# Two gate tiles by seven products, later reloads in a down projection, and a rearranged end in a one-layer decoder step

## The chip, the cores and the metric

The kernel runs on one core of a Trainium2 chip. A core has a matrix engine (TensorE, PE in the rows), a vector engine (VectorE, DVE), an activation engine (ScalarE, ACT), GpSimd (POOL), and SyncE (SP), whose queue issues most of the transfers between the chip's main memory and the core's on-chip memory. The engines run their own instruction lists in order and meet only at semaphores. The metric is the device time of one execution in microseconds (us), as the median of several; lower is better.

## The reference: what is computed

One layer of a decoder is applied to 16 meta tokens and 512 prompt tokens, and to 8 running sequences of 4 tokens each (32 sample tokens): 560 columns in all, with 1024 features. The layer is a half-step SwiGLU network, a mixer, and a second half-step SwiGLU network, each between two normalisations. Cut to what matters:

```python
h = x + 0.5 * rms_norm(swiglu(rms_norm(x, g1), w_gate, w_up, w_down), post1)
u = rms_norm(h, mix_pre_g)
q_a, k_a, v_a, gk_low, r_a, q_b, k_b, v_b, gate_a, gate_b = split(u @ w_in)
o_a = rms_norm(gla(q_a, k_a, v_a, gk_low), gla_norm_g) * silu(r_a)
o_b = stick_breaking_attention(q_b, k_b, v_b, cached pages)
m = sigmoid(gate_a) * (o_a @ w_o_gla) + sigmoid(gate_b) * (o_b @ w_o_sb)
h = h + rms_norm(m @ w_out, mix_post_g)
y = h + 0.5 * rms_norm(swiglu(rms_norm(h, g2), w_gate2, w_up2, w_down2), post2)
```

The hidden width is 2816. Cached keys and values lie in pages of 128 tokens, two for each sequence, found through a page table.

## The kernel before

**Layout.** Activations are held transposed: 128 features in the partitions, tokens in the columns. A weight tile is 128 output features by 1024 input features, which is eight 128x128 blocks. All products are made to nearly full float32 precision out of a rounded part (hi) and a remainder (lo) of both operands: hi*hi + hi*lo + lo*hi, three matmuls for each block. ScalarE makes the hi of a weight chunk (`Chunks.split`, L661, or `parted`, L959) and VectorE the lo (`tt`, whose one line is L153). Three buffers of each kind rotate: `raw` as it comes from memory, `hi` and `lo`. A raw buffer is free for the next transfer when its lo is made.

**Plain and seven-product tiles.** A plain tile ("R", `tile_steps`, L682 to L685) runs eight steps of six matmuls, the columns cut in two halves of 280 and 264. A pair of tiles can instead be made together by a Strassen-Winograd scheme ("S", `seven_steps`, L1028 to L1030): the weights of the pair are four quarters, VectorE makes four sums of them (`weight_sums`), sums of activation quarters are used beside the plain quarters, and seven products of 12 matmuls (272 columns) replace eight. Products 1 to 4 go to four accumulators a, d, b, c; products 5, 6 and 7 are added onto a, d and c. Before that, ScalarE has to copy a and d out, and VectorE has to add c into the sum called v. Four further adds make the pair's results. The first network and the second use the same scheme for most tiles, and so does one pair of each down product (`Down.pair`).

**Steps.** The code is written as a list of PE steps. `later(n, f)` puts f behind the n-th step from now; `when(n, f)` puts it behind step n of a stage. So the order of the instructions on PE, VectorE, ScalarE and GpSimd is written by hand; SyncE's order is set by a planner. Within a step the `later` work stands ahead of the `when` work.

**Rooms.** On-chip buffers come from an arena (`take`, `give`) that knows only the order of the program: a room taken again makes its new user wait for the last reader of the old one.

**The first down product** (`order1`, L1624 on). After two plain tiles comes the seven-product pair 2 and 3, then the first column halves of tiles 4 to 7, 22 steps of three matmuls each, then the second halves of tiles 7 to 4. Each tile's weights come as three chunks of 512, 448 and 448 KB. Right behind the pair, `h_again(8)` reloads the residual h, which was parked in memory, as eight transfers of 280 KB, one every eight steps (L1294). `EARLY = {4: 2}` fetches one 512 KB chunk of `w_in` ahead of its time when tile 4 starts (L634). The residual is first used when the first halves are normalised, 13 steps after tile 7's first half.

**The mixer's end** (`MIXER`, L2525 on). Steps 0 to 40 are r gates, 40 to 104 the product `o_a @ w_o_gla` (tiles o), then plain gate tiles a0 and a1 (8 steps each, `gate_a`), then S pairs and p tiles. Meanwhile the sampled tokens' attention uses pages gathered by GpSimd (`page`, L2069) into twelve rooms of a list `ring`; used pages go back to `ring`, and its rooms go back to the arena at step 113. `sample_out` copies its result out at steps 117 and 119 (16 small VectorE copies, L2254). The activation sums that the S pairs need were parked in memory: `sums_back` reloads them (L2342), at the steps of `SUMS_BACK`, and ScalarE and VectorE split them 8 to 12 steps later. From two steps after b0 starts, `obs` splits (L2348; a ScalarE rounding and a VectorE remainder each) follow every four steps.

**The end** (`Last.end`). Behind the last product, 256 prompt rows and the 32 sample rows remain. PE turns them by transposes, sums of squares are made by ones-matmuls (L855, L856), ScalarE makes the scale (L857, L858), VectorE scales and adds, and SyncE writes out. `tt(..., eng)` is `Last.add`'s helper; it takes VectorE unless told otherwise.

Of the kernel before, what the change touches and what calls it, by code (L numbers as in the profile page):

```python
# [121 lines left out]
def hybrid_step(  # L122
# [579 lines left out]
    GATES, ROWS, EARLY = 6, 1, {4: 2}  # L702
# [69 lines left out]
    class Last:  # L772
# [9 lines left out]
        def tile(self, n, h, acc):  # L782
# [13 lines left out]
            S.activation(q, acc[:, :w], AF.Square)  # L796
            y = self.view(g)[:, n % 3, c]
            if h and self.n[h] == KD:
                V.tensor_scalar(out=y, in0=acc[:, :w], scalar1=self.post[:, n : n + 1], scalar2=None, op0=ALU.mult)
            else:  # L800
                S.activation(y, acc[:, :w], AF.Copy, scale=self.post[:, n : n + 1])
# [13 lines left out]
        def add(self, g, c, rs):  # L815
            n = len(Norm.SETS[g])
            y, x = self.view(g)[:, :, c], hT_room[g].rearrange("p (k t) -> p k t", t=NT)[:, :n, c]
            tt(y, y, rs.unsqueeze(1).to_broadcast([P, n, c.stop - c.start]), ALU.mult)
            tt(x, x, y, ALU.add)

        def end(self, prompt, samples):
            def turned(src, c, n, w):
                p = ps("acc")
# [10 lines left out]
            def x_turned(c):  # L834
                t = take(D)
                for w in range(2):
                    p = ps()
                    for i in range(4):
                        T.transpose(p[:, P * i : P * i + P], hT[4 * w + i][:, c : c + P], ident)
                    S.copy(t[:, 512 * w : 512 * w + 512], p)  # L840
                return t
# [7 lines left out]
            q, rs = self.q["sum"], take(P)  # L849
# [4 lines left out]
            for i, c in enumerate((A, B)):  # L854
                T.matmul(p[:, i : i + 1], q[:, c : c + P], ones[:, :1], start=True, stop=True)  # L855
            T.matmul(p[:, 2 : 2 + NS], ones, q[:, C:NW], start=True, stop=True)  # L856
            S.activation(rs[:, : 2 + NS], p[:, : 2 + NS], AF.Ln, bias=epst, scale=1.0 / D)  # L857
            S.activation(rs[:, : 2 + NS], rs[:, : 2 + NS], AF.Exp, scale=-0.5)  # L858
            ya.append(turned(y_at, A, P, 1))
            out(A, 0, ya[0], xa, rs[:, 0:1])  # L860
            xb = x_turned(B)
            out(A, 1, ya[1], xa, rs[:, 0:1])
            for g in range(3):
                self.add(g, slice(C, NW), rs[:, 2 : 2 + NS])
            yb = [turned(y_at, B, P, w) for w in range(2)]
            pc = [turned(x_at, C, NS, w) for w in range(2)]
            out(B, 0, yb[0], xb, rs[:, 1:2])
            for w in range(2):
                t = take(512)
                S.copy(t[:NS], pc[w][:NS])  # L870
                nc.sync.dma_start(samples[:, 512 * w : 512 * w + 512], t[:NS])
            out(B, 1, yb[1], xb, rs[:, 1:2])
# [417 lines left out]
    def h_again(every):  # L1290
        nonlocal hT_room
        hT[:], hT_room = whole(KD)
        for k in range(KD):
            later(1 + every * k, lambda k=k: nc.sync.dma_start(hT[k], h_dram[k]))  # L1294
# [163 lines left out]
    with tc.manual_schedule(engines={E.PE, E.DVE, E.Activation, E.Pool}):  # L1458
# [607 lines left out]

    def page(src, i, c):
# [44 lines left out]
    def sample_keys(b, q, kp, kT):  # L2112
# [8 lines left out]
        if q:  # L2121
            ring.extend((kp[b, 0], kp[b, 1]))
# [88 lines left out]
    def sample_values(c, b0, vp, oz):  # L2211
# [8 lines left out]
        ring.extend(vp.values())  # L2220
# [83 lines left out]
    def gate_a(n):  # L2304
        acc = yield from tile_steps(um, W1)
        sg = take(NW)

        def sig():
            for h in range(2):
                S.activation(sg[:, h * HW : h * HW + W2[h]], acc[h][:, : W2[h]], AF.Sigmoid)  # L2310

# [390 lines left out]
```

## Time and profile before

| | |
|---|---|
| median of 3 runs | 1506.71 us (1506.67 to 1508.04) |
| the profiled execution: its time | 1508.72 us |
| its span, first to last instruction | 1507.0 us |
| PE busy | 1494.2 us of the span (99%) |
| VectorE busy | 1090.0 us (72%) |
| ScalarE busy | 771.5 us (51%) |
| GpSimd busy | 149.3 us (10%) |
| mean granted PE clock | 0.999 of full speed |
| data moved | 180.4 MB, mean 120 GB/s |

In timeline rows the columns are start, duration, engine, line, operation, output and inputs, shape and count, and in brackets the idle time before it and who ended it. Matmuls are pipelined, so their pace is read from the distance of two starts and not from a duration. In rows of windows the columns are the stretch, its length, busy time and instruction count of PE, weight loads, VectorE, ScalarE and GpSimd, then the granted PE clock, the busy share of the transfer engines and GB/s.

### The profile page before, as it was taken

What the parts mean: (1) busy time and instruction counts of PE and PEld (TensorE: products, weight loads), DVE (VectorE), ACT (ScalarE), POOL (GpSimd) and SP (SyncE); (2) the same over time, 40 slices, a digit from 0 to 9 for tenths busy, and PEclk for the clock granted to TensorE, in tenths of its full rate; (3) what the DMA queues carried; (4) which work ended last, traced back from release to release, by engine and by line L of the source; (5) the groups of instructions that cost most, each with busy time, mean ns of one, the idle gap of its engine ahead of it and who ended that gap; (6) DMA issues with size and microseconds to landing.
All of it is one profiled execution on the core that took longest, in us unless ns stands there. A gap on an engine that the chain in (4) does not pass through costs nothing.

```text
span 1507.0 us, 29698 instructions
## 1 busy us (share of the span) xinstructions
PE 1494.2 (99%) x11941; PEld 1442.1 (96%) x11941; DVE 1090.0 (72%) x1939; ACT 771.5 (51%) x1422; POOL 149.3 (10%) x216
## 2 busy tenths in 40 slices
PE   9999999999999999999999999999999999999998
PEld 8999999999999889999888899999999999999998
DVE  5888888853787866877776534977567898888544
ACT  6545454533655556565555343634564555455334
POOL 2000000000000011123324551000000000000000
PEclk9999999999999999999999999999999999999999
DMA  8123333336565473335555568335532233333352
GB/s 250 55 86 99 99 98 97 88 101 195 147 160 148 122 112 85 91 82 118 131 105 139 169 204 192 105 96 144 152 103 79 85 111 99 99 99 89 86 168 98
DMA packets 276458, 180.40 MB, mean 120 GB/s; under 512 B 10154, under 2 KB 260736, under 8 KB 276320
## 3 DMA queue, kind: packets, MB, share of 16 engines
q1 hardware_dynamic: 270864, 161.64, 40.6%
q0 software_dynamic: 5440, 16.85, 3.2%
q8 instruction: 94, 1.54, 0.4%
q14 instruction: 44, 0.36, 0.1%
q10 hardware_dynamic: 16, 0.00, 0.0%
HBM read 155.72 MB, written 22.74 MB: 118 GB/s over the span
## 4 chain that ended last, share of the span: by engine, by line
PE 94%; DVE 2%; DMA 2%; ACT 1%; issue 0%; DVEq 0%; SPq 0%; ACTq 0%
PE acc L682 8%; PE acc L1248 8%; PE acc L1249 8%; PE acc L685 8%; PE acc L683 8%; PE acc L1250 8%; PE acc L695 7%; PE acc L698 7%; PE acc L696 7%; PE acc L1191 2%; PE acc L1188 2%; PE acc L1189 2%; PE acc L1028 1%; PE acc L1029 1%; PE acc L1030 1%; PE ps L2023 1%
## 5 line engine op out<-in xcount | busy, mean ns | idle before, releaser
L153 DVE TENSOR_TENSOR lo<-raw,hi 128x1024 fp32r<-128x1024 f32 (+1 forms) x213 | 254.9, 1197 | 125.9 <-ACT hi L661 102.5
L153 DVE TENSOR_TENSOR room<-room,room 128x544 f32<-128x544 f32 (+17 forms) x413 | 259.0, 649 | 81.4 <-ACT room L740 15.0
L682 PE MATMUL acc<-room,hi 128*128 128x280 f32 (+1 forms) x928 | 271.2, 309 | 0.2 <-DVE room L156 0.2
L1249 PE MATMUL acc<-room,hi 128*128 128x280 f32 (+1 forms) x896 | 259.3, 289 | 0.0
L1248 PE MATMUL acc<-room,hi 128*128 128x280 f32 (+1 forms) x896 | 259.3, 289 | 0.0
L1250 PE MATMUL acc<-room,lo 128*128 128x280 f32 (+1 forms) x896 | 259.1, 289 | 0.0
L683 PE MATMUL acc<-room,hi 128*128 128x280 f32 (+1 forms) x928 | 250.3, 289 | 0.1
L685 PE MATMUL acc<-room,lo 128*128 128x280 f32 (+1 forms) x928 | 192.8, 289 | 0.0
L682 PEld LDWEIGHTS acc<-room,hi 128*128 128x128 f32 x928 | 174.7, 188 | 13.1 <-issue 11.0
L683 PEld LDWEIGHTS acc<-room,hi 128*128 128x128 f32 x928 | 175.0, 189 | 2.8 <-issue 1.9
L1248 PEld LDWEIGHTS acc<-room,hi 128*128 128x128 f32 x896 | 168.6, 188 | 0.0
L1250 PEld LDWEIGHTS acc<-room,lo 128*128 128x128 f32 x896 | 168.6, 188 | 0.0
L1249 PEld LDWEIGHTS acc<-room,hi 128*128 128x128 f32 x896 | 168.4, 188 | 0.0
L959 ACT CAST hi<-raw 128x1024 fp32r<-128x1024 f32 x92 | 96.4, 1052 | 133.1 <-PE acc L1249 48.8
L661 ACT CAST hi<-raw 128x1024 fp32r<-128x1024 f32 (+1 forms) x121 | 122.7, 1015 | 72.0 <-DMA raw<-in_ffn_w_down_dram 18.6
L685 PEld LDWEIGHTS acc<-room,lo 128*128 128x128 f32 x928 | 145.0, 188 | 0.0
L695 PE MATMUL acc<-room,hi 128*128 128x280 f32 (+2 forms) x498 | 143.7, 296 | 0.9 <-ACT hi L661 0.9
L696 PE MATMUL acc<-room,hi 128*128 128x280 f32 (+2 forms) x498 | 141.5, 292 | 0.0
L698 PE MATMUL acc<-room,lo 128*128 128x280 f32 (+2 forms) x498 | 128.4, 292 | 0.7 <-DVE lo L153 0.7
L959 ACT CAST hi<-room 128x1024 fp32r<-128x1024 f32 x84 | 70.2, 836 | 80.8 <-PE acc L1249 60.3
L695 PE MATMUL acc<-room,room 128*128 128x280 f32 (+3 forms) x366 | 107.8, 295 | 0.0
L153 DVE TENSOR_TENSOR lo<-room,hi 128x1024 fp32r<-128x1024 f32 x84 | 80.2, 955 | 36.7 <-ACT hi L959 36.5
(406 smaller groups left out, 3299.5 us busy)
## 6 DMA issues: line engine op xcount, KB each, us to landing
raw<-in_w_in_dram SPq DMA_DIRECT2D x49, 512.0 KB
raw<-in_ffn_w_down_dram SPq DMA_DIRECT2D x40, 448.0 KB
raw<-in_ffn_w_gate_dram SPq DMA_DIRECT2D x64, 256.0 KB
raw<-in_ffn_w_up_dram SPq DMA_DIRECT2D x64, 256.0 KB
out_dram<-room SPq DMA_DIRECT2D x36, 256.0 KB
raw<-in_ffn_w_down_dram SPq DMA_DIRECT2D x14, 512.0 KB
raw<-in_w_in_dram SPq DMA_DIRECT2D x28, 256.0 KB
h_dram<-room SPq DMA_DIRECT2D x24, 280.0 KB
```

The lines of the kernel that those rows point to most:

```text
L153: (eng or V).tensor_tensor(out=out, in0=a, in1=b, op=op)
L661: S.copy(h_, src)
L682: T.matmul(acc[h][:, : wid[h]], hi[k], a[h][0], start=(k == 0), stop=False)
L683: T.matmul(acc[h][:, : wid[h]], hi[k], a[h][1], start=False, stop=False)
L685: T.matmul(acc[h][:, : wid[h]], lo[k], a[h][0], start=False, stop=(k == KD - 1))
L695: T.matmul(acc[h][:nw, : wid[h]], wh, a[h][0], start=(k == 0), stop=False)
L696: T.matmul(acc[h][:nw, : wid[h]], wh, a[h][1], start=False, stop=False)
L698: T.matmul(acc[h][:nw, : wid[h]], wl, a[h][0], start=False, stop=(k == kt - 1))
L959: S.copy(hi[:, :kt], src)
L1248: T.matmul(x[:, :QW], hi, act[k][0], start=(first and k == 0), stop=False, skip_group_check=True)
L1249: T.matmul(x[:, :QW], hi, act[k][1], start=False, stop=False, skip_group_check=True)
L1250: T.matmul(x[:, :QW], lo, act[k][0], start=False, stop=(k == 3), skip_group_check=True)
```

## The change

- Gate tiles a0 and a1 become one S pair; the mixer is two steps shorter from there. `gate_a` goes. As no gate needs them any more, halves of the plain activations are given back when tile o0 starts (`halved`).
- `SUMS_BACK` moves from steps 80, 88, 96, 104 to 70, 78, 86, 92.
- Page rooms are given to the arena one by one once nothing is left to gather (`back`).
- In the first down product the eight loads of h start at step 24 and come every 11 steps; the early chunk of `w_in` is fetched when tile 5 starts. In the second one the loads of h start at step 8 and come every 5 steps.
- In the end, the sums of squares over all but the last tile are summed across partitions first, and the last tile's are added in PSUM by three further matmuls in place of a VectorE add. The sample rows are scaled and added on GpSimd; their transposes, copies and writes come last, and the writes are issued by ScalarE's queue.

```diff
-SUMS_BACK = (80, 88, 96, 104)
+SUMS_BACK = (70, 78, 86, 92)
-MIXER += [("R", "o", n) for n in range(8)] + [("R", "a", 0), ("R", "a", 1), ("S", "b", 0), ("S", "a", 2), ("S", "b", 2), ("R", "p", 0), ("R", "p", 1)]
+MIXER += [("R", "o", n) for n in range(8)] + [("S", "a", 0), ("S", "b", 0), ("S", "a", 2), ("S", "b", 2), ("R", "p", 0), ("R", "p", 1)]
...
-    GATES, ROWS, EARLY = 6, 1, {4: 2}
+    GATES, ROWS, EARLY = 6, 1, {5: 2}
...
-        def add(self, g, c, rs):
+        def add(self, g, c, rs, eng=None):
...
-            tt(y, y, rs.unsqueeze(1).to_broadcast([P, n, c.stop - c.start]), ALU.mult)
-            tt(x, x, y, ALU.add)
+            tt(y, y, rs.unsqueeze(1).to_broadcast([P, n, c.stop - c.start]), ALU.mult, eng)
+            tt(x, x, y, ALU.add, eng)
...
+            def x_turned(t, c, w):
+                S.copy(t[:, 512 * w : 512 * w + 512], turned(x_at, c, P, w, ps()))
+
+            def sums(p, q, first):
+                for i, c in enumerate((A, B)):
+                    T.matmul(p[:, i : i + 1], q[:, c : c + P], ones[:, :1], start=first and i == 0, stop=False, skip_group_check=True)
+                T.matmul(p[:, 2 : 2 + NS], ones, q[:, C:NW], start=False, stop=not first, skip_group_check=True)
...
-            xa = x_turned(A)
-            tt(q[:, A:NW], q[:, A:NW], self.q["last"][:, A:NW], ALU.add)
-            ya = [turned(y_at, A, P, 0)]
...
+            sums(p, self.q["sum"], True)
+            x_turned(xa, A, 0)
+            sums(p, self.q["last"], False)
             S.activation(rs[:, : 2 + NS], p[:, : 2 + NS], AF.Ln, bias=epst, scale=1.0 / D)
             S.activation(rs[:, : 2 + NS], rs[:, : 2 + NS], AF.Exp, scale=-0.5)
-            ya.append(turned(y_at, A, P, 1))
-            out(A, 0, ya[0], xa, rs[:, 0:1])
-            xb = x_turned(B)
-            out(A, 1, ya[1], xa, rs[:, 0:1])
             for g in range(3):
-                self.add(g, slice(C, NW), rs[:, 2 : 2 + NS])
+                self.add(g, slice(C, NW), rs[:, 2 : 2 + NS], G)
+            x_turned(xa, A, 1)
+            ya = [turned(y_at, A, P, w) for w in range(2)]
+            for w in range(2):
+                out(A, w, ya[w], xa, rs[:, 0:1])
+                x_turned(xb, B, w)
             yb = [turned(y_at, B, P, w) for w in range(2)]
-            pc = [turned(x_at, C, NS, w) for w in range(2)]
-            out(B, 0, yb[0], xb, rs[:, 1:2])
...
-                t = take(512)
-                S.copy(t[:NS], pc[w][:NS])
-                nc.sync.dma_start(samples[:, 512 * w : 512 * w + 512], t[:NS])
-            out(B, 1, yb[1], xb, rs[:, 1:2])
+                out(B, w, yb[w], xb, rs[:, 1:2])
+            for w in range(2):
+                p, t = turned(x_at, C, NS, w), take(512)
+                S.copy(t[:NS], p[:NS])
+                nc.scalar.dma_start(samples[:, 512 * w : 512 * w + 512], t[:NS])
...
-    def h_again(every):
+    def h_again(first, every):
...
-            later(1 + every * k, lambda k=k: nc.sync.dma_start(hT[k], h_dram[k]))
+            later(first + every * k, lambda k=k: nc.sync.dma_start(hT[k], h_dram[k]))
...
-                later(2, lambda: h_again(8))
+                later(2, lambda: h_again(24, 11))
...
+    def back(*ts):
+        if asked:
+            ring.extend(ts)
+        else:
+            give(*ts)
...
-            ring.extend((kp[b, 0], kp[b, 1]))
+            back(kp[b, 0], kp[b, 1])
...
-        ring.extend(vp.values())
+        back(*vp.values())
...
-            for h in range(2):
+            for h in range(1 if k < 4 else 2):
...
+        def halved():
+            for k in range(4):
+                parts_ = [arena.halves(t) for t in um.full[k]]
+                give(*(t[1] for t in parts_))
+                um.full[k] = [t[0] for t in parts_]
+
+        when(starts["o", 0] + 1, halved)
...
-                    later(2, lambda: h_again(5))
+                    later(2, lambda: h_again(8, 5))
```

More of the change, by code (lines that the diff above doesn't have):

```diff
@@ L832, in y_at @@
                 return self.view(k // 3)[:, k % 3]
[L834 to L841, printed above, removed]
+            def x_turned(t, c, w):
[4 more added lines that the diff above has]
+                T.matmul(p[:, 2 : 2 + NS], ones, q[:, C:NW], start=False, stop=not first, skip_group_check=True)
             def out(c, w, y, x, r):
@@ L2302, in gate_r @@
         later(4, lambda: split(oas, n, o, oap))
[L2304 to L2308, printed above, removed]
-            for h in range(2):
-                S.activation(sg[:, h * HW : h * HW + W2[h]], acc[h][:, : W2[h]], AF.Sigmoid)
-        def by():
-            tt(m1[n], sg, m1[n], ALU.mult)
-            give(sg)
-        later(1, sig)
-        later(3, by)
     def gate_pair(what, n):
@@ L2359, in sums_lo @@
         for k in (i, i + 4):
-            for h in range(2):
+            for h in range(1 if k < 4 else 2):
                 c = slice(QW * h, QW * h + QW)
@@ L2568, in hybrid_step @@
         when(starts["p", 6] + 2, h_back)
[L2569 removed]
+        mains = {"r": gate_r, "o": out_a, "p": product_b}
+        def halved():
[4 more added lines that the diff above has]
+        when(starts["o", 0] + 1, halved)
         n = 0
```

13 lines of the change are left out of this document (5 added, 8 removed).

## The prediction

> **What bounds the kernel now.** The page comes first: its busy shares and the chain that ended last.
>
> ```profile
> PE 1494.2 (99%) x11941; PEld 1442.1 (96%) x11941; DVE 1090.0 (72%) x1939; ACT 771.5 (51%) x1422; POOL 149.3 (10%) x216
> PE 94%; DVE 2%; DMA 2%; ACT 1%; issue 0%; DVEq 0%; SPq 0%; ACTq 0%
> ```
>
> PE is busy for 1494.2 of 1507.0 us and carries 94% of the chain. So there are only three things to win: fewer matmuls, the few places where PE waits, and the end, where it has nothing left. But a mean of 72% for VectorE says nothing of a stage in which it is full. The change touches one place of each sort, so I read the stretches next: the list of waits, windows of 10 us over the whole span for the count of matmuls, then the timeline wherever the count drops.
>
> The largest drop is in the first down product. These rows are from the chain, PE's timeline, SyncE's timeline, and 2 us windows:
>
> ```profile
> 333.59 8.34 DMA raw<-in_ffn_w_down_dram
> ...
> 341.91 0.30 PE L698 MATMUL acc<-room,lo 128*128 128x280 f32 x1
> 343.11 0.40 PE L695 MATMUL acc<-room,hi 128*128 128x280 f32 x1 [0.90 <-ACT hi L661]
> 343.34 0.29 PE L696 MATMUL acc<-room,hi 128*128 128x280 f32 x1
> 344.37 0.40 PE L698 MATMUL acc<-room,lo 128*128 128x280 f32 x1 [0.73 <-DVE lo L153]
> ...
> 331.30 0.43 SPq L634 DMA_DIRECT2D room<-in_w_in_dram  x1
> 331.77 0.50 SPq L1294 DMA_DIRECT2D room<-h_dram  x1
> 333.59 0.37 SPq L186 DMA_DIRECT2D raw<-in_ffn_w_down_dram  x1
> 334.00 1.75 SPq L1294 DMA_DIRECT2D room<-h_dram  x1
> ...
> 346.00:348.00 2.00, 2.00 (x11) 2.00 (x10) 1.43 (x3) 1.23 (x3) 0.00 (x0) 0.50 0.95 271
> 348.00:350.00 2.00, 2.00 (x14) 2.00 (x14) 0.58 (x2) 1.05 (x1) 0.00 (x0) 0.73 0.87 276
> ```
>
> Tile 5's first chunk was issued at 333.59, among the early `w_in` chunk and the first loads of h, and took 8.34 us. PE's starts are 0.13 us apart here; the gaps at 343.11 and 344.37 are longer by 1.07 and 0.90, so PE idles 1.97 us. Then the granted clock is 0.50: 11 and 14 matmuls in 2 us where 16 fit, and from 345.6 to 349.1 some 1.6 us more are lost. This place costs 3.6 us in the profiled execution.
>
> **First part: later loads in the first down product.** No instruction is added. At 333.59 neither h nor the `w_in` chunk is in the way any more, and the chunk had 6.0 us: it must land by 339.6 to be split (1.05 us on ScalarE, 1.23 on VectorE) before 341.9. Nothing else is new on SyncE's queue there, so I expect it in 4 us and the stall gone. What comes next: in tile 5's 8.5 us (22 steps of 3 x 0.128) the weights' 1408 KB, the 512 KB chunk and two loads of h are 2480 KB, 290 GB/s, and the windows above show 271 to 276 moved at a busy share near 0.9. That is close to full. But steady chunks are issued two tiles' thirds ahead and have some 8 us each. Bounds: nothing (the stall comes back one tile later) and -3.6; I take **-3.6**. The last load of h is now at step 103 after the pair and is read at step 141, 38 steps or 15 us later, so lateness there costs nothing. The shift by seven steps in the second down product is counted as nothing: its last load is at step 45 and is read at 73. If either cover were gone, PE would wait for one 280 KB load.
>
> **Second part: a0 and a1 as one S pair.** On PE, 96 matmuls with 272 columns on average become 84. These are PE rows around the seventh products of b0 and a2, and VectorE's rows ahead of it:
>
> ```profile
> 958.53 0.29 PE L1029 MATMUL acc<-room,hi 128*128 128x272 f32 x1
> 958.66 0.29 PE L1030 MATMUL acc<-room,lo 128*128 128x272 f32 x1
> 958.98 0.39 PE L1028 MATMUL acc<-room,hi 128*128 128x272 f32 x1
> ...
> 969.48 0.29 PE L1030 MATMUL acc<-room,lo 128*128 128x272 f32 x1
> 970.05 0.40 PE L1028 MATMUL acc<-room,hi 128*128 128x272 f32 x1 [0.28 <-DVE room L153]
> ...
> 947.29 3.25 DVE L2254 COPY room<-ps 64x32 f32<-64x32 f32 x16
> 950.58 1.23 DVE L153 TENSOR_TENSOR lo<-room,hi 128x1024 fp32r<-128x1024 f32 x1
> ...
> 952.86 1.35 DVE L153 TENSOR_TENSOR room<-room,room 128x544 f32<-128x544 f32 x2
> 954.13 0.68 DVE L153 TENSOR_TENSOR room<-raw,raw 128x512 f32<-128x512 f32 x1
> ...
> 956.18 0.69 DVE L153 TENSOR_TENSOR lo<-room,hi 128x512 fp32r<-128x512 f32 x1
> 956.78 0.68 DVE L153 TENSOR_TENSOR room<-raw,room 128x512 f32<-128x512 f32 x1
> 957.50 0.44 DVE L153 TENSOR_TENSOR room<-room,acc 128x272 f32<-128x272 f32 x1
> 957.85 0.72 DVE L153 TENSOR_TENSOR room<-room,room 128x544 fp32r<-128x544 f32 x1
> 958.49 0.43 DVE L153 TENSOR_TENSOR room<-room,acc 128x272 f32<-128x272 f32 x1
> ```
>
> At 0.125 us a matmul the 12 that go are worth 1.5 us. But the last row is b0's v, and PE's seventh product starts right behind it, 0.2 us late. VectorE has been full since 947.29: before this change too it is what PE meets here. The new pair adds four weight sums, more lo work and five adds. Most of that lands ahead of step 104, where VectorE has gaps, and the earlier `SUMS_BACK` takes its remainders out of this stretch. What does not move are the two adds c12 and c21 of the new pair: c12 reads its sixth product, stands at step 117, and everything behind it in VectorE's list waits.
>
> So I sum VectorE's list from a0's sixth product to b0's v, each by the distance of starts above. c12 0.35, the sample copies 3.25, two lo's 1.14 each (950.58 to 952.86 holds two), c21 0.35, two gate products and an `obs` remainder 0.64 each, three weight sums 2.05 (954.13 to 956.18), the quarter's lo 0.60, the fourth sum 0.72, u2 0.35, another `obs` remainder 0.64, v 0.43: 12.9 us. In that time PE has a0's seventh product and six of b0's, 84 x 0.125 = 10.5 us. It will wait about **2.5 us** where it waited 0.2. The part is then -1.5 + 2.3 = +0.8 us. Bounds: -1.5 if the wait does not come, +3 if it does and a2's weights follow late.
>
> A wait of that length may also cost the clock. The rows above show half clock behind 1.97 us of idle time. Smaller waits at one place of the attention, 1.08 us in the window below, left the clock at 1.00:
>
> ```profile
> 842.00:844.00 2.00, 0.92 (x14) 0.41 (x17) 0.05 (x1) 0.00 (x0) 0.68 (x1) 1.00 0.63 207
> ```
>
> 2.5 us lies above the larger, so I count two chances in three for 1.6 us lost, less the 0.45 us wait in a2 at 970.05 that a slower PE would no longer meet: +0.7 on average. The part stands at **+1.5**.
>
> By the Trainium skill ("TensorE: Matmul & The Clock Gate", What's actually happening) the clock falls to half only after an idle window of some 3.4 us. Taken literally, a wait of 2.5 us leaves the clock alone and the part at +0.8. The trace differs: 1.97 us in two pieces was enough at 343.
>
> `halved` and `back` run no instruction; they change which room is taken and so which old reader is waited for, which I count as nothing within 0.5 us. The sums' eight loads move ahead of two weight fetches; that is a rival below.
>
> **Third part: the end.**
>
> ```profile
> 1495.64 1.04 PE L839 MATMUL ps<-ident,room 128*128 128x128 f32 x8
> ...
> 1497.28 0.58 PE L855 MATMUL ps<-ones,room 128*128 128x1 f32 x4 [0.17 <-DVE room L153]
> 1497.72 0.39 PE L856 MATMUL ps<-room,ones 128*128 128x32 f32 x2
> ...
> 1498.14 0.29 ACT L857 ACTIVATE room<-ps,epst 128x34 f32<-128x34 f32 x1 [0.80 <-PE ps L856]
> ...
> 1498.73 1.41 DVE L156 SCALAR_TENSOR_TENSOR room<-acc,room,room 128x512 f32<-128x512 f32 x2 [1.60 <-ACT room L858]
> 1500.05 1.39 DVE L153 TENSOR_TENSOR room<-room,room 128x96 f32<-128x96 f32 x6
> 1501.37 1.40 DVE L156 SCALAR_TENSOR_TENSOR room<-acc,room,room 128x512 f32<-128x512 f32 x2
> ...
> 1503.68 0.36 SPq L846 DMA_DIRECT2D out_dram<-room  x1
> ```
>
> Now PE starts with sums (0.66, from 1497.28 to the next group at 1497.94), four transposes (0.44, half of 1495.64 to 1496.51), sums again: 1497.4, so the scale's first step comes at 1497.6 and not 1498.14. Five groups of four transposes and two more follow to 1500.4. VectorE's last prompt product ends near 1501.6 instead of 1502.8, since the sample adds (1.39) left its list. SyncE then writes at 1501.7 rather than 1503.68, where the last write stood behind the sample rows' writes: -2.0.
>
> The sample rows decide whether that holds. GpSimd's cost of a 128x96 float product is shown nowhere; the nearest rows:
>
> ```profile
> L153 POOL TENSOR_TENSOR idx<-pidx,rowi 128x16 int32<-128x16 int32 x2 | 0.4, 220 | 0.1
> L1930 POOL TENSOR_SCALAR_AFFINE_SELECT room<-room 128x128 f32<-128x128 f32 x64 | 43.3, 698 | 146.3 <-ACT room L1926 145.7
> ```
>
> Six operations at 0.22 to 0.70 take 1.3 to 4.2 us; I take 0.4 each, between them, 2.4 us from 1498.2. Then eight transposes and two copies put the last sample write at about 1502.8, 0.9 earlier than the last write before. It is smaller (64 KB), so the end gains between 0.9 and 2.0: **-1.5**, with -2.0 and +0.9 as bounds.
>
> The Trainium skill ("GPSIMD Engine Reference", 3.1 Elementwise) has 2.6 cycles for an element of a two-input operation; by it 96 elements are an estimated 0.2 us plus dispatch, near the value taken.
>
> **Sum.** -3.6 + 1.5 - 1.5 = -3.6 us. Against the profiled execution (1508.72) that is 1505.1; against the median (1506.71, which is 2.0 lower) 1503.1. What the profiled execution has more is not shown. If it is the half clock at 346, the first part is worth only 2.0 in most runs; so I keep the upper part of the range wide.
>
> **Rivals.**
> - The wait in b0 does not come, because rooms or the planner put VectorE's work elsewhere: -3.6 - 1.5 - 1.5 = -6.6, 1500.1. For it: the planner's order and the rooms after the change cannot be seen in this trace. Against: c12 cannot start before a0's sixth product.
> - The late weights return one tile later, at 290 GB/s: the first part gives nothing, 1506.7.
> - The end gains nothing because GpSimd is slow or its writes land last: 1504.6.
> - Slower: the sums' loads block SyncE. In the list of its waits:
>
> ```profile
> SPq L2342 <- DVE room L153: 9.3, 2, 8.0
> SPq L2342 <- PE ps L2218: 5.8, 1, 5.8
> ```
>
> One of these loads already held the queue for 8.0 us, hidden by weights that were two tiles ahead (a tile takes 6.0 us). Issued ten steps earlier, into rooms that pages have just left, the two waits may fall together: 13.8 us, less the 8.0 that are covered, is 5.8 of PE waiting and 1.6 of clock: 1510.5. It decides once one wait passes about 8 us and then some 6 more.
>
> **Chances.** My forecast (1503.1, its own range 1501.5 to 1504.5) 0.46, of which 0.36 lies below 1503.7; no wait in b0 0.22; late weights 0.11; no gain at the end 0.07; blocked queue 0.14. A difference within 0.2%, 3.0 us, is about what a measurement of this kernel can tell from none: faster 0.36 + 0.22 = 0.58, same 0.10 + 0.11 + 0.07 = 0.28, slower 0.14. The range 1499.8 to 1506.9 leaves out the blocked queue and little else.
>
> **What would show it.** First part right: no drop below 31 matmuls in 4 us between 336 and 360, clock 1.00, no wait for `in_ffn_w_down`. Second: 84 matmuls for a0, VectorE without a gap from a0's sixth product, a wait of 2 to 3 us at L1028 in b0 released by VectorE, and perhaps 0.50 clock behind it. Third: L857 half a microsecond closer to the last product, four prompt writes on SyncE's queue, six GpSimd rows, and sample writes last on ScalarE's. I am wrong if b0's wait is missing, if PE waits for weights of tiles o, or if the last write is later than 8 us behind the last product.

## The result, and the profile after

The changed kernel is slower: 1509.74 us median of 20 runs (1508.06 to 1512.27), against 1507.15 us for the kernel before in the same series (20 runs, 1506.47 to 1508.05). The ratio is 1.0016 with a 95% interval of 1.001 to 1.0023, so +2.4 us (1.5 to 3.5). The prediction was 1503.1 us with a range up to 1506.9: the sign is wrong.

The page's busy line and the chain by engine, after:

```profile
PE 1493.7 (99%) x11935; PEld 1442.7 (96%) x11935; DVE 1095.5 (73%) x1943; ACT 773.7 (51%) x1425; POOL 151.8 (10%) x222
PE 96%; DVE 2%; ACT 1%; DMA 0%; issue 0%; ACTq 0%; DVEq 0%; SPq 0%
```

TensorE still bounds everything. To see where time went I cut the span at instructions that all programs have. The view of one line gives its first and last start; for the last product of the seven-product scheme before (L1028) and after (L1026), and the last turning of cached keys (L2118, L2122):

```profile
L2118 PE MATMUL ps<-ident,room x128: 270/272/273, 707.5 to 889.3; 128*128 128x128 f32 x128
L1028 PE MATMUL acc<-room,hi x196: 283/288/398, 949.8 to 1060.2; 128*128 128x272 f32 x196
...
L2122 PE MATMUL ps<-ident,room x128: 270/272/273, 704.7 to 886.4; 128*128 128x128 f32 x128
L1026 PE MATMUL acc<-room,hi x224: 282/288/597, 933.2 to 1060.4; 128*128 128x272 f32 x112
```

From 889.3 to 1060.2 is 170.9 us before; from 886.4 to 1060.4 is 174.0 after. The same for three other stretches gives a table that I use for every run below:

| profiled execution | down 1 | mixer | network 2 | end | median, us |
|---|---|---|---|---|---|
| before | 141.5 (half clock) | 170.9 | 167.8 | 47.5 | 1507.15 |
| after | 139.1 | 174.0 (half clock) | 168.4 | 47.8 | 1509.74 |

"Down 1" runs from the first product of the first down pair (L1412 before, L1410 after) to the first turning of values in the recurrence (L357); "mixer" is the stretch just worked out; "network 2" runs from the last start of L1187 to the last of L1246; "end" from the last product of the second down pair (L1412, L1410) to the last instruction. (The expectations below call the keys' turning "the last transpose of the recurrence", the down pair "the gather product" or "the sixth group before the end", and L357 "the attention's"; the lines and numbers are those of the table.) At 322 us the changed kernel was 0.5 us ahead, by chance as far as I can see; the stretches that the table leaves out agree within 0.2 us.

The first down product after: chain, TensorE, SyncE and a 2 us window.

```profile
333.08 7.52 DMA raw<-in_ffn_w_down_dram
...
341.40 0.30 PE L698 MATMUL acc<-room,lo 128*128 128x280 f32 x1
341.78 0.39 PE L695 MATMUL acc<-room,hi 128*128 128x280 f32 x1
...
343.04 0.40 PE L698 MATMUL acc<-room,lo 128*128 128x280 f32 x1 [0.74 <-DVE lo L153]
...
330.40 0.81 SPq L1292 DMA_DIRECT2D room<-h_dram  x2
331.31 0.38 SPq L634 DMA_DIRECT2D room<-in_w_in_dram  x1
333.08 0.38 SPq L186 DMA_DIRECT2D raw<-in_ffn_w_down_dram  x1
333.51 0.57 SPq L1292 DMA_DIRECT2D room<-h_dram  x1
...
346.00:348.00 2.00, 2.00 (x18) 2.00 (x17) 1.09 (x2) 0.68 (x1) 0.00 (x0) 1.00 0.75 206
```

SyncE still issues two loads of h and the early `w_in` chunk right ahead of the weight chunk, and a third load right behind it. The chunk takes 7.52 us where it took 8.34. TensorE's start at 341.78 is 0.25 us late and the one at 343.04, whose predecessor starts at 342.01, 0.90 us: 1.15 us of waiting are left of 1.97, and the half clock is missing.

The mixer after: TensorE, VectorE, then windows.

```profile
954.35 0.29 PE L1028 MATMUL acc<-room,lo 128*128 128x272 f32 x1
957.27 0.60 PE L1026 MATMUL acc<-room,hi 128*128 128x272 f32 x1 [2.64 <-DVE room L153]
957.67 0.43 PE L1027 MATMUL acc<-room,hi 128*128 128x272 f32 x1
...
944.13 0.44 DVE L153 TENSOR_TENSOR room<-room,acc 128x272 f32<-128x272 f32 x1 [0.88 <-PE acc L1028]
...
947.74 1.60 DVE L2258 COPY room<-ps 64x32 f32<-64x32 f32 x8
956.79 0.43 DVE L153 TENSOR_TENSOR room<-room,acc 128x272 f32<-128x272 f32 x1
...
956.00:958.00 2.00, 0.73 (x3) 0.73 (x4) 2.00 (x4) 0.82 (x1) 0.00 (x0) 0.63 0.14 41
958.00:960.00 2.00, 2.00 (x11) 2.00 (x11) 2.00 (x5) 0.00 (x0) 0.00 (x0) 0.50 0.12 26
960.00:962.00 2.00, 2.00 (x11) 2.00 (x11) 1.91 (x3) 1.83 (x3) 0.00 (x0) 0.50 0.55 134
962.00:964.00 2.00, 2.00 (x13) 2.00 (x13) 1.81 (x3) 1.03 (x3) 0.00 (x0) 0.66 0.36 82
```

The wait in b0 is there, 2.64 us, released by VectorE's v at 956.79, and the clock is at half from then to about 963. The row at 944.13 is c12, the first add behind a0's sixth product. From its start to the end of v at 957.22 VectorE has no gap: 13.1 us of list, where the prediction added up 12.9.

The end after, on ScalarE, GpSimd, SyncE and ScalarE's queue, and half-microsecond windows behind it (last column GB/s):

```profile
1498.15 0.29 ACT L855 ACTIVATE room<-ps,epst 128x34 f32<-128x34 f32 x1
1498.84 2.28 POOL L153 TENSOR_TENSOR room<-room,room 128x96 f32<-128x96 f32 x6 [579.74 <-ACT room L856]
1499.90 2.74 SPq L847 DMA_DIRECT2D out_dram<-room  x4
1503.32 0.32 ACTq L870 DMA_DIRECT2D out_dram<-room  x1
...
1504.50:1505.00 0.50, 0.00 (x0) 0.00 (x0) 0.00 (x0) 0.00 (x0) 0.00 (x0) 1.00 0.18 57
1505.00:1505.50 0.50, 0.00 (x0) 0.00 (x0) 0.00 (x0) 0.00 (x0) 0.00 (x0) 1.00 0.00 0
```

The bytes have all moved by about 1504.6, the last instruction is at 1508.0: 3.4 us. In the kernel before, half a window had bytes from 1505.0 on and the end came at 1507.0, some 1.7 us behind them:

```profile
1505.00:1505.50 0.50, 0.00 (x0) 0.00 (x0) 0.00 (x0) 0.00 (x0) 0.00 (x0) 1.00 0.51 193
```

### The profile page after: what moved, and what is told of

It is laid out like the page before. It is cut to its first block, busy times and chain, and to the rows that moved or that the text cites. A ratio compares the mean times of both kernels' runs of the same rounds, so it can differ in the third digit from the quotient of the medians.

```text
span 1508.0 us, 29714 instructions
## 1 busy us (share of the span) xinstructions
PE 1493.7 (99%) x11935; PEld 1442.7 (96%) x11935; DVE 1095.5 (73%) x1943; ACT 773.7 (51%) x1425; POOL 151.8 (10%) x222
## 4 chain that ended last, share of the span: by engine, by line
PE 96%; DVE 2%; ACT 1%; DMA 0%; issue 0%; ACTq 0%; DVEq 0%; SPq 0%
PE acc L682 8%; PE acc L1246 8%; PE acc L1248 8%; PE acc L1247 8%; PE acc L683 7%; PE acc L685 7%; PE acc L695 7%; PE acc L698 7%; PE acc L696 7%; PE acc L1026 2%; PE acc L1028 2%; PE acc L1027 2%; PE acc L1189 2%; PE acc L1186 2%; PE acc L1187 2%; PE ps L2021 1%
## 5 line engine op out<-in xcount | busy, mean ns | idle before, releaser
L153 DVE TENSOR_TENSOR room<-room,room 128x544 fp32r<-128x544 f32 (+17 forms) x405 | 255.9, 656 | 65.3 <-ACT room L761 14.4
L682 PE MATMUL acc<-room,hi 128*128 128x280 f32 (+1 forms) x896 | 262.2, 310 | 0.2 <-DVE room L156 0.2
L1248 PE MATMUL acc<-room,lo 128*128 128x280 f32 (+1 forms) x896 | 259.4, 290 | 0.0
L1247 PE MATMUL acc<-room,hi 128*128 128x280 f32 (+1 forms) x896 | 259.4, 290 | 0.0
L1246 PE MATMUL acc<-room,hi 128*128 128x280 f32 (+1 forms) x896 | 259.4, 289 | 0.0
L683 PE MATMUL acc<-room,hi 128*128 128x280 f32 (+1 forms) x896 | 241.7, 289 | 0.1
L685 PE MATMUL acc<-room,lo 128*128 128x280 f32 (+1 forms) x896 | 186.1, 289 | 0.0
L682 PEld LDWEIGHTS acc<-room,hi 128*128 128x128 f32 x896 | 168.7, 188 | 12.9 <-issue 10.8
L683 PEld LDWEIGHTS acc<-room,hi 128*128 128x128 f32 x896 | 169.0, 189 | 2.7 <-issue 1.9
L1248 PEld LDWEIGHTS acc<-room,lo 128*128 128x128 f32 x896 | 168.8, 188 | 0.0
L1246 PEld LDWEIGHTS acc<-room,hi 128*128 128x128 f32 x896 | 168.6, 188 | 0.0
L1247 PEld LDWEIGHTS acc<-room,hi 128*128 128x128 f32 x896 | 168.4, 188 | 0.0
L685 PEld LDWEIGHTS acc<-room,lo 128*128 128x128 f32 x896 | 139.9, 188 | 0.0
```

The costliest lines, as they stand in the source:

```text
L153: (eng or V).tensor_tensor(out=out, in0=a, in1=b, op=op)
L682: T.matmul(acc[h][:, : wid[h]], hi[k], a[h][0], start=(k == 0), stop=False)
L683: T.matmul(acc[h][:, : wid[h]], hi[k], a[h][1], start=False, stop=False)
L685: T.matmul(acc[h][:, : wid[h]], lo[k], a[h][0], start=False, stop=(k == KD - 1))
L1246: T.matmul(x[:, :QW], hi, act[k][0], start=(first and k == 0), stop=False, skip_group_check=True)
L1247: T.matmul(x[:, :QW], hi, act[k][1], start=False, stop=False, skip_group_check=True)
```

## The experiments

My theory after the result: the first part does nothing because SyncE's order hardly changed, the second costs what it looks like, and the end is held by something behind the last bytes. Rivals stand in the expectations.

**One part at a time.** Three kernels each take one part of the change into the kernel before. The edits are the diff's own; the shortest is the loads':

```diff
-    GATES, ROWS, EARLY = 6, 1, {4: 2}
+    GATES, ROWS, EARLY = 6, 1, {5: 2}
...
-                later(2, lambda: h_again(8))
+                later(2, lambda: h_again(24, 11))
...
-                    later(2, lambda: h_again(5))
+                    later(2, lambda: h_again(8, 5))
```

> The kernel before with the load edits of the change alone (h from step 24, every 11; the early chunk with tile 5; h from step 8 in the second down product). Theory A, the planner ignores the steps: in the trace of after SyncE still issues h at 330.4, 333.5 and 338.9 us, so the wait near 342 stays between 1 and 2 us, and the time is that of before within 0.7 us (1506.5 to 1507.5). Rival, the step positions count: no wait near 342, 2 us or more faster (1505).

> The kernel before with the S pair a0/a1, the earlier SUMS_BACK, the given-back halves and page rooms, and nothing else. Theory B, VectorE's list makes PE wait: a wait of 2.6 us at L1028 in b0 and half clock behind it for some 6 us (2.6 us lost), less 1.5 for the matmuls and 0.45 for the wait in a2 that goes: +3.2 us, 1510.4. Rival, the pair is worth its 12 matmuls and the loss sits elsewhere: -1.5, 1505.7.

> The kernel before with the new end alone. Theory C, the end gives nothing: in the traces the last product's end to the last instruction is 11.4 us before and 11.7 us after, so 0 to +1 us: 1507.2 to 1508.2. Rival, the end is worth what was forecast and the profiled execution hides it: -1.5, 1505.7.

| kernel | down 1 | mixer | network 2 | end | median, us | ratio to before |
|---|---|---|---|---|---|---|
| loads only | 141.3 (half clock) | 170.9 | 168.3 | 47.5 | 1507.88 | 1.0004 (0.9994 to 1.0013) |
| pair only | 139.4 | 172.9 (half clock) | 168.1 | 47.7 | 1509.17 | 1.0012 (1.0003 to 1.0021) |
| end only | 139.5 | 170.9 | 167.8 | 47.9 | 1507.42 | 0.9999 (0.999 to 1.0008) |

The kernel before stood at 1507.16 in this series. The pair alone carries most of the loss; the loads and the end gain nothing. "Down 1" says something else that I had not looked for: pair only and end only have the old loads and yet take 139.4 and 139.5, two less than the execution I had predicted from. Loads only has the new loads and shows the old picture:

```profile
343.26 0.40 PE L695 MATMUL acc<-room,hi 128*128 128x280 f32 x1 [0.76 <-ACT hi L661]
344.52 0.40 PE L698 MATMUL acc<-room,lo 128*128 128x280 f32 x1 [0.73 <-DVE lo L153]
...
346.00:348.00 2.00, 2.00 (x10) 2.00 (x10) 1.45 (x3) 1.43 (x3) 0.00 (x0) 0.50 0.84 251
```

So an execution with either order of the loads can have the half clock behind 342 us or lack it. How often it comes may still depend on the loads: 3 of the 11 executions of loads only have a mean granted clock of 0.998, the others 0.999 or 1.000, and of the kernel before in the same series 1 of 33 has 0.998. The mean is a rough sign: it does not say where the clock was lost, and a short drop can vanish in its rounding (0.999 in the profiled execution of the kernel before).

**Copies of the sample rows to ScalarE.** The changed kernel with `sample_out`'s sixteen copies on ScalarE:

```diff
-                V.tensor_copy(ob[pr][r_, NP : NP + NS].rearrange("p (b t) -> p b t", t=4),
+                S.copy(ob[pr][r_, NP : NP + NS].rearrange("p (b t) -> p b t", t=4),
```

> The changed kernel with the 16 small copies of sample_out on ScalarE instead of VectorE. Theory B: VectorE's list from a0's sixth product to b0's v shrinks from 12.9 to 9.7 us, less than PE's 10.5, so the wait at L1026 in b0 falls from 2.6 to under 0.3 us, the clock stays at 1.00, and 5 us come back less some 0.5 that a2 waits again: 1505 (1504 to 1506). Rival, the wait is set by something behind VectorE's list (weights from memory, ScalarE): the wait stays above 1.5 us and the time near 1509.7.

Measured: 1508.21 us, ratio 1.0007 (0.9998 to 1.0016); mixer 170.9, clock 1.00, and this wait:

```profile
951.74 1.36 DVE L153 TENSOR_TENSOR room<-room,room 128x544 f32<-128x544 f32 x2 [0.70 <-ACT room L2314]
...
957.74 0.40 PE L1026 MATMUL acc<-room,hi 128*128 128x272 f32 x1 [1.59 <-DVE room L153]
```

Taking 3.2 us off VectorE shortened the wait by 1.05 only. VectorE now waits for ScalarE instead: 0.56 us ahead of 946.65, for a weight's hi that the copies used to hide, and 0.95 ahead of 949.18 and 0.70 ahead of 951.74, for work that stands behind the copies in ScalarE's list (1.55 us from 946.52, 1.52 us from 949.73). Together that is 2.2 us, which is what is missing. What went is the wait's 1.05 and the half clock, and in the mixer the pair then breaks even with the kernel before. The 1505 of the expectation was too low.

**Half of the copies later.** Eight of the sixteen move fourteen products on:

```diff
-            when(n + 1 + 2 * i, sample_out, i)
+            when(n + (1, 3, 5, 21)[i], sample_out, i)
```

> The changed kernel with the last eight copies of the samples' sums (1.6 us on VectorE) fourteen products later, behind the wait. On VectorE they stand ahead of the result that b0's seventh product waits for. Theory A (VectorE's list ahead of that result is what is late): the wait falls from 2.6 to 1.0, no half clock follows, and the stage from the last transpose of the recurrence to the last of the seven products falls from 174.0 to 170.0 to 170.6, below the 170.9 of the kernel before; total 1506.0 to 1506.8. Rival (what VectorE waits for from ScalarE is late anyway, as in the run with the copies on ScalarE, where 1.6 of wait were left): wait 1.6 to 2, stage 170.9 to 171.5, total 1507 to 1508.

Measured: 1508.03 us, ratio 1.0004 (0.9994 to 1.0013), mixer 171.0. The wait in b0 fell as expected, and a new one came 12 us later, in a2:

```profile
956.24 0.39 PE L1026 MATMUL acc<-room,hi 128*128 128x272 f32 x1 [0.88 <-DVE room L153]
...
968.33 0.40 PE L1026 MATMUL acc<-room,hi 128*128 128x272 f32 x1 [1.28 <-DVE room L153]
```

The work moved and most of the wait moved with it: 2.16 us are left in the two places, and the clock stayed up.

**Work for TensorE during the wait.** Products of ones into a spare bank, ahead of b0's seventh product; nothing reads them.

```diff
+            if f == ("b", 0) and key == "t4":
+                filler = ps()
+                for _ in range(20):
+                    T.matmul(filler[:, :P], ones, ones, start=True, stop=True)
```

> The changed kernel with twenty products of ones into a spare bank ahead of b0's seventh product, so that TensorE works while it waits for VectorE; the results of the twenty are used nowhere. In the changed kernel TensorE waits 2.6 us there and its clock is then at half for some 6 us. From the last transpose of the recurrence (L2122) to the last of the seven products (L1026) it takes 174.0 us, the kernel before 170.9. Theory A (the half clock follows from the idle time and is worth more than the wait): the clock stays at 1.00, the stage takes 171.2 to 171.8, the total is 2.2 to 2.8 below the changed kernel, so 1507 to 1507.5. Rival (the half clock costs the 1.1 us that my prediction gave it, and the rest of the stage's 3.1 is VectorE's): the stage takes 173, the total is about 1508.6.

Measured: 1509.98 us, ratio 1.0016 (1.0006 to 1.0025), mixer 172.9 with the clock at 1.00. Twenty were too many: they kept TensorE 4.4 us (next start 959.66) where the wait is 2.64, so neither expectation is decided.

```profile
955.27 4.63 PE L1027 MATMUL ps<-ones 128*128 128x128 f32 x40
```

With twelve:

> As the run with twenty products of ones, but with twelve: the twenty took 4.4 us where the wait is 2.6 and so added what they saved. Twelve take 2.6. Theory A (the clock drops because TensorE idles): clock 1.00 there in every execution, the stage from L2122's last start to L1026's last 171.3 to 171.8, total 0.8 to 1.4 below the changed kernel's median, whose executions differ by 2.2 between the stage with and without the half clock. Rival (the clock has nothing to do with it): the stage shows half clock in about two executions of three as without them, total unchanged at 1509.5 to 1510.

Measured: 1508.69 us, ratio 1.0013 (1.0003 to 1.0023), range 1507.78 to 1509.28 instead of 1508.06 to 1512.27; mixer 171.7, and the clock stays up:

```profile
955.43 2.85 PE L1027 MATMUL ps<-ones 128*128 128x128 f32 x24
...
958.00:960.00 2.00, 2.00 (x17) 1.87 (x16) 2.00 (x4) 0.10 (x1) 0.00 (x0) 1.00 0.00 0
960.00:962.00 2.00, 2.00 (x18) 2.00 (x18) 2.00 (x4) 2.00 (x3) 0.00 (x0) 1.00 0.38 93
```

TensorE waits just as long for the result, but working. The stretch and the smaller spread are as theory A has them. So is the mean clock of the single executions: all ten have 0.999 or 1.000, like the eleven of end only, which has the same end and no long wait, while 13 of the changed kernel's 20 have 0.997 or 0.998. The medians' difference, 1.05, is from two series whose kernel before differs by 0.64 (1507.15 and 1506.51); the 0.4 that is left is less than the intervals of the two ratios can tell.

**The sample rows' writes on SyncE.**

```diff
-                nc.scalar.dma_start(samples[:, 512 * w : 512 * w + 512], t[:NS])
+                nc.sync.dma_start(samples[:, 512 * w : 512 * w + 512], t[:NS])
```

> The changed kernel with the two writes of the samples issued from SyncE instead of ScalarE. In the changed kernel the last bytes move about 3 us before the last instruction, in the kernel before about 1.6; from the first product of the sixth group before the end (L1410's last) to the end it takes 47.8 against 47.5. Theory A (a write from ScalarE's queue is reported done later): last byte to end 1.6 to 2.0, this stretch 46.3 to 46.8, total 1.0 to 1.4 below the changed kernel. Rival (the time behind the last byte is that of the last small write, whatever its queue): 47.6 to 48, total unchanged at 1509.5 to 1510.

Measured: 1508.96 us, ratio 1.0011 (1.0002 to 1.0021), end 47.9. The queue makes no difference. This execution gave something else, the same wait without half clock, mixer 171.8:

```profile
958.43 0.39 PE L1026 MATMUL acc<-room,hi 128*128 128x272 f32 x1 [2.65 <-DVE room L153]
...
960.00:962.00 2.00, 2.00 (x18) 2.00 (x17) 2.00 (x4) 1.89 (x3) 0.00 (x0) 1.00 0.36 82
```

**GpSimd late in the kernel before.** One GpSimd copy more:

```diff
-            out(B, 1, yb[1], xb, rs[:, 1:2])
+            last = out(B, 1, yb[1], xb, rs[:, 1:2])
+            G.tensor_copy(take(P)[:, :8], last[:, :8])
```

(`out` returns its tile `o` for it.)

> The kernel before with one instruction more: at its end GpSimd copies 8 columns of the last prompt tile into a tile that nobody reads, so that GpSimd works about as late as VectorE does. In the kernels with the changed end the last instruction stands 6.9 to 7.0 us behind the end of GpSimd's six operations and 3.3 to 3.4 us behind the last bytes, in the kernel before, where GpSimd had been idle for long, 1.5 us behind the last bytes. Theory A (the program's end waits for GpSimd, which takes long to finish after late work): the copy ends near 0.4 us behind VectorE's last operation, the end comes 6.9 to 7.0 us behind that, so from L1410's last start to the end 49.5 to 50.2 instead of 47.5, total 2.0 to 2.6 above the kernel before. Rival (it is the last write of the samples' rows that lands late, GpSimd has no part in it): 47.5, total unchanged.

Measured: 1509.35 us, ratio 1.0019 (1.0009 to 1.0028), end 50.6 instead of 47.5. GpSimd's row, the last window with bytes, and the span:

```profile
1500.37 0.19 POOL L874 COPY room<-room 128x8 f32<-128x8 f32 x1 [581.69 <-DVE room L156]
...
1503.00:1503.50 0.50, 0.00 (x0) 0.00 (x0) 0.00 (x0) 0.00 (x0) 0.00 (x0) 0.50 0.01 4
...
core 0: 1507.5 us, clock 0.998
```

The copy ends at 1500.56, the program 6.94 us later, over 4 us behind the last bytes. In the changed kernel the six operations end at 1501.12 and the program at 1508.0, 6.9 us later. A copy of 0.19 us that nobody reads costs the whole kernel 3 us.

**The six operations on VectorE again**, in the changed end behind the first prompt half:

```diff
-            for g in range(3):
-                self.add(g, slice(C, NW), rs[:, 2 : 2 + NS], G)
...
+            for g in range(3):
+                self.add(g, slice(C, NW), rs[:, 2 : 2 + NS])
             yb = [turned(y_at, B, P, w) for w in range(2)]
```

> The changed kernel with the six operations on the samples' rows on VectorE, behind the first half of the prompt as in the kernel before, and none on GpSimd; the writes stay in the changed order and on ScalarE's queue. VectorE's last operation is then some 1.1 us later than in the changed kernel. Theory A (GpSimd's late work holds the end): the end comes 1.5 to 2 us behind the last bytes, from L1410's last start to the end 46.8 to 47.5 instead of 47.8. Rival (the samples' writes land late): 3.3 us stay behind the last bytes, 48.8 to 49.2.

Measured: 1508.98 us, ratio 1.0018 (1.0008 to 1.0027), end 47.3, inside theory A's range, with 1.8 us behind the last bytes (1507.2 to 1509.0) in place of 3.4:

```profile
1507.00:1507.50 0.50, 0.00 (x0) 0.00 (x0) 0.00 (x0) 0.00 (x0) 0.00 (x0) 0.50 0.30 111
1507.50:1508.00 0.50, 0.00 (x0) 0.00 (x0) 0.00 (x0) 0.00 (x0) 0.00 (x0) 0.50 0.00 0
```

**Loads of h that really move.** The kernel before, with the first down product's loads of h issued by ScalarE, whose list follows the steps (`h_again` takes the engine as an argument for it):

```diff
-                later(2, lambda: h_again(8))
+                later(2, lambda: h_again(24, 11, nc.scalar))
```

> The kernel before with the loads of h for the first down product issued by ScalarE, and later, at places that really delay them; in the change SyncE issued them as early as before. The stretch from the first gather product (L1410's first) to the first of the attention's transposes (L357's first) takes 139.1 to 139.7 where the clock stays up behind 342 us, and 141.3 to 141.5 where it drops. Theory A, that of my prediction (h's loads stand in the way of the weights there): ScalarE's wait for the weights goes, no drop of the clock, stretch 138.0 to 138.8, total 0.7 to 1.3 below the kernel before. Rival (the waiting is for the conversion of the weights as such and for chance in their landing): stretch 139 to 140, total 1507 to 1507.5, the same as before; if the extra issues delay ScalarE, up to 1 slower.

Measured: 1505.27 us, ratio 0.9984 (0.9974 to 0.9993), down 1 137.8. SyncE's rows, ScalarE's split of tile 5's first chunk, and the window where TensorE waited:

```profile
331.06 0.37 SPq L634 DMA_DIRECT2D room<-in_w_in_dram  x1
333.61 17.84 SPq L186 DMA_DIRECT2D raw<-in_ffn_w_down_dram  x8
...
339.24 1.05 ACT L661 CAST hi<-raw 128x1024 fp32r<-128x1024 f32 x1 [2.50 <-DMA raw<-in_ffn_w_down_dram]
342.70 0.36 ACTq L1294 DMA_DIRECT2D room<-h_dram  x1
...
342.00:344.00 2.00, 2.00 (x18) 2.00 (x17) 1.05 (x2) 1.38 (x3) 0.00 (x0) 1.00 0.49 135
```

The split starts at 339.24 instead of 342.01 or 340.68, inside the 339.6 that the prediction asked for, and the wait is gone. It is theory A with a little more than expected. Two more kernels ask whether it is the loads' time or their place, and whether the gain holds beside the end without GpSimd:

```diff
-                later(2, lambda: h_again(24, 11, nc.scalar))
+                later(2, lambda: h_again(1, 8, nc.scalar))
```

> The kernel with h's loads on ScalarE's queue, but at the early steps of the kernel before (the first after one step, then every eight) instead of 24 and every eleven. There the wait at 342 us was gone and the stretch from L1410's first start to L357's first took 137.8 instead of 139.1 to 141.5. Theory A (the loads themselves are in the weights' way, so it is their time that counts): the wait returns at least in part, 0.4 to 1.0 in front of L695 and 0.7 in front of L698, the stretch takes 139 to 140, total 0.2 below the kernel before to 0.2 above. Rival (it is SyncE's queue: without h's eight issues SyncE reaches the weights sooner, whenever h is loaded): no wait, stretch 137.6 to 138.2, total 1.8 to 2.2 below the kernel before.

> The kernel with h's loads late on ScalarE's queue, and with the changed end, whose six operations on the samples' rows are VectorE's. The end with VectorE took 47.3 from L1410's last start where the kernel before takes 47.5. If the two add up: 1.9 to 2.5 below the kernel before, the stretch behind 322 us 137.6 to 138.2, the end 47.2 to 47.4. Rival: the gain by h's loads was chance in the weights' landing, and a second program with the same loads shows the wait again: total within 0.5 of the kernel before.

Measured: 1504.57 us, ratio 0.9988 (0.9979 to 0.9997), down 1 137.8, for the early loads; 1504.89 us, ratio 0.9991 (0.9982 to 1.0), down 1 137.8, end 47.7, with the changed end. The kernel before stood at 1506.40. In the early one ScalarE issues the first load of h at 335.90, among the weights, and nothing waits:

```profile
333.80 15.70 SPq L186 DMA_DIRECT2D raw<-in_ffn_w_down_dram  x7
...
335.90 0.36 ACTq L1294 DMA_DIRECT2D room<-h_dram  x1
...
342.00:344.00 2.00, 2.00 (x18) 2.00 (x17) 0.95 (x2) 1.22 (x2) 0.00 (x0) 1.00 1.00 279
```

So loads of h on ScalarE's queue beside the weights are harmless; what hurts is loads on SyncE's queue around the chunk, two ahead of it and one right behind. Which of the three did it was not separated. Nor was the queue from the order: ScalarE's early loads start only behind the chunk, and no run sends loads of h ahead of it from another queue. In their own series the three programs are 2.2, 1.8 and 1.5 us below the kernel before, the third with an interval that reaches 1.0. The changed end adds nothing.

## Why the prediction was wrong

**First part, -3.6: failed, twice.** The step that failed is "At 333.59 neither h nor the `w_in` chunk is in the way any more". I read the order of SyncE's queue off the steps, though it is a planner that sets it: after the change two loads of h and the chunk still go out at 330.40 to 331.31, and the weights still take 7.52 us. That h's loads on SyncE's queue delay the weights was right, as the loads issued by ScalarE show; that the `w_in` chunk does was not, for in that run it still goes out ahead of them, at 331.06, and nothing waits. The second failure is the size. Of the 3.6 some 1.6 were half clock, and a typical execution of the kernel before does not have it: executions of either kernel without the drop take 139.1 to 139.9 there, with it 141.3 to 141.9, and without any wait 137.8. Of the kernel before, the series of the single parts had 2 runs of 33 above 1508.3. I had even named this ("If it is the half clock at 346, the first part is worth only 2.0 in most runs"), kept 3.6 in the sum, and subtracted it from a median that did not contain it. Taking the loads off SyncE's queue is worth some 1.8 us in this stretch. This change is worth nothing that can be told there: without half clock the stretch takes 139.1 to 139.9 with the new loads and 139.4 to 139.7 with the old ones (pair only, end only, GpSimd late). For the profiled execution it is -0.3, 139.1 against the 139.4 of pair only.

**Second part, +1.5: right in mechanism and nearly in size.** VectorE's list gave a wait of 2.5 us, measured 2.64, and taking 1.6 us off the list shortened the wait by 1.76 (half of the copies later). Without half clock the mixer takes 171.8 instead of 170.9: +0.9, forecast +0.8. With it 172.7 (the run with VectorE's sample adds), 172.9 and 174.0, so the drop costs 0.9 to 2.2 us when it comes, forecast 1.6. It lasted up to 6 us here and not 3.5. The pair alone measured 1.0012, +1.8 us. The forecast took two chances in three for the drop; three of the four profiled executions with the full wait and no filler had it. By the mean clock, 0.998 or less, it was 13 of 20 executions of the changed kernel, 8 of 11 of pair only, and 2 of 10 with the samples' writes on SyncE, so how often it comes may differ from program to program.

By the Trainium skill ("TensorE: Matmul & The Clock Gate", What's actually happening) the clock falls after an idle window of some 3.4 us, and the window runs free, so that one program can meet it at different places. The second half fits: the same 2.6 us wait brought half clock in three executions and none in a fourth. The first half does not: waits of 0.76 and 0.73 us, one behind the other, were enough in loads only, and 0.84 and 0.73 were not in the run with twelve fillers. At 0.65 and 0.73 or less no profiled execution showed a drop.

**Third part, -1.5: the writes were right, the end was not.** The scale is ready early (1498.15, 1.85 us behind the last product's group at 1496.30, before 2.50), GpSimd's six operations took 0.38 us each (taken 0.4), and the last bytes land by 1504.6. With the 1.7 us that lay behind the bytes before, that would have been 1506.3, an estimate of 46.1 from the second down pair against 47.5: -1.4. What failed is the unspoken step that the program ends when the last write lands. It ends 6.9 us after GpSimd's last instruction if that is later, and this takes back the 1.4 and 0.3 more: 47.8. Without GpSimd the operations are back in VectorE's list, and the end gains as little: 47.3 and 47.7 in the two programs that have it so.

**What stays open.** Network 2 takes 168.4 after and 167.8 before, spread evenly: TensorE's count in the same 166 us is

```profile
1196.00:1362.00 166.00, 166.00 (x1332) 166.00 (x1331) 145.89 (x221) 83.82 (x129) 0.00 (x0) 1.00 0.35 101
...
1196.00:1362.00 166.00, 166.00 (x1327) 166.00 (x1326) 145.77 (x221) 83.92 (x129) 0.00 (x0) 1.00 0.35 101
```

The clock is at 1.00 and no wait is listed. Loads only (168.3) and pair only (168.1) have it, end only and the kernels with ScalarE's loads (167.8) do not. I counted nothing for it, and found no cause.

The sum by measured terms: -0.3 or nothing for the loads, +0.9 for the pair, +0.3 for the end, +0.6 in network 2 make +1.5 to +1.8. The ratio says +2.4. What is left is most likely half clock, and the executions' mean clocks bear it out: the 7 of the changed kernel's 20 with 0.999 or 1.000 have a median of 1508.61, 1.5 above the kernel before, the 13 with less 1509.77, 2.6 above. One of the 7 took 1511.11, which stays unexplained.

Of the rivals, "late weights return" and "the end gains nothing" have the terms that were measured, for other reasons than I gave. One of the sums' loads held SyncE's queue for 8.4 us, but TensorE waited for no weights behind it.

## What to carry to other kernels

A transfer that is written later in the program is later only if the list of its queue says so; where a planner orders the queue, issue it from an engine whose order is written by hand. A term measured in one execution is to be subtracted from that execution's time: look first whether the typical run has it, above all where half clock is part of it. Before work is moved to an idle engine near the end, ask how long the program takes to end behind that engine.

## What the hardware showed that I had not expected

- The program ended 6.9 to 7.0 us after GpSimd's last instruction in each profiled execution where GpSimd worked in the last 10 us (eight programs), and 1.7 and 1.8 us after the last bytes in the two where I looked and it did not. Adding one copy of 0.19 us cost 3.1 us in the end.
- Half clock comes by chance at waits of 1.5 to 2.6 us: the same wait of 2.6 us was followed by none, some 3 us or 6 us of it in four programs. Twelve products without use in the wait kept the mean clock at 0.999 or 1.000 in ten executions of ten.
- Loads of 280 KB in one queue with a weight chunk, two ahead of it and one right behind, delayed it by up to 2.8 us (the split at 342.01 instead of 339.24); issued from another queue behind the chunk they delayed nothing that TensorE waited for.
